# Pacing the weight-sum transfers of a recurrence stage, and issuing their copies from another engine

## The chip, the core and the metric

The kernel runs on one core of a Trainium2 chip. The metric is the device time of one execution in microseconds. The kernel before was timed three times: 2056.03, 2061.7 and 2062.01 us, median 2061.7 us.

## The reference

Two layers work on 1024 tokens of 1024 channels. The first layer mixes tokens with a gated linear recurrence (HGRN2) of eight heads, the second with a causal convolution; each is followed by a squared-ReLU MLP, and every step ends in a scaled residual and a layer norm. The part that matters here is the recurrence and the MLP's second weight:

```
q = silu(x @ Wq);  f = lb + (1-lb)*sigmoid(x @ Wf);  k = 1-f;  v = x @ Wv
S_t = diag(f_t) S_{t-1} + k_t v_t^T;    o_t = S_t^T q_t          # per head, 128 x 128 states
o = o * rsqrt(mean(o^2) + eps) * norm_g                          # per head and token
o = o * silu(x @ Wg);  mix = o @ w_out
x = layer_norm(ALPHA*x + mix)
x = layer_norm(ALPHA*x + square(relu(x @ w1)) @ w2)
```

## The kernel before

Matrices are multiplied in float32 by splitting each operand into a high and a low part (three matmuls for one), and large products are done by a seven-product scheme on 2 x 2 blocks, which needs sums and differences of the weight's blocks beside the blocks themselves. The second MLP weights `w2` of both layers are cut into 16 pieces of four 128 x 1024 blocks (`to_sum`, L427). For each piece `block_sums` (L399 to L426) makes four sums in DRAM with transfers alone, and they are read back as weight forms much later (`form`, L429, from 871.6 us on in the trace).

For a piece that is summed during the recurrence stage there are five transfers, all issued by GpSimd. Two plain copies of 1 MB put blocks into the four sum places (L419 and L420). An adding transfer of 1 MB (L421) adds two more blocks onto the first two places, and so needs the first copy to have landed. Two adding transfers of 512 KB (both L423) add one sum place onto the next, so each needs the transfer before it. A transfer that needs another waits for it on GpSimd, at its issue, and what GpSimd has behind it in its order waits too. With `gap=12` the five are recorded at ticks 0, 6, 12, 24 and 36.

The order of work in this stage is written out by the code itself (`manual_schedule`, L372): the engines' instructions stand in the order in which the Python code issues them. Twelve pairs of weight columns, seven block products each (the loop at L1007), make 84 products of 12 matmuls. `pair_product` calls `slot` after every three matmuls; `slot` calls `tick` (L390), which counts one tick and runs the jobs that `later` (L384) has put down for it. So a tick is a step of recording, not a time. `make_form` (L587) prepares weight forms in `fs` about three products ahead: ScalarE rounds to the high part, VectorE subtracts. `evacuate` (L824) empties a product's PSUM bank, on ScalarE by `COPY t<-ps` for three of the seven; the bank of such a product is next written one product later at the earliest.

Between products, `step` (L883) advances up to two of the eight heads through `recurrence(h)` (L634). Its last steps matter here. `outer` and `chain` make the states, `attend` leaves a head's output in PSUM in two halves (`out_ps`), and `settle(half)` (L731) normalises one: four squares with sums on ScalarE (`o,ss<-ps`, L735), two small instructions on GpSimd (`ss`, L736 and L518: scale and add, then the power -1/2), and four ticks later four scalings on ScalarE (`o<-ps,ss`, L741). `give(half)` (L746) then turns the half with four transposes on TensorE (`ps<-ident,o`) and stores it. So each half of each head makes a round ScalarE, GpSimd, ScalarE, TensorE, and GpSimd's part stands in one order with the sum transfers.

SyncE issues all other loads and stores of the stage, among them 256 KB weight blocks (`pr`, L585). In the main loop a new piece of `to_sum` is begun when `(7 * p + ORDER.index(i)) % 6 == 1`, every sixth product, as long as more than four pieces are left (L1022 and L1023): twelve pieces. The other four are done later, two from L1442 and two from L1774.

Of the kernel before, what the change touches and what calls it, by code (L numbers as in the profile page):

```python
# [12 lines left out]
ALU = mybir.AluOpType  # L13
# [21 lines left out]
NPAR = TAP + KB * TAPS  # L35

KBYTES = 220
PAIRS = [("q", 0), ("q", 1), ("q", 2), ("q", 3), ("g", 0), ("q", 4), ("q", 5), ("q", 6), ("g", 1), ("q", 7), ("g", 2), ("g", 3)]
NPOOL = (12, 11)
SEQ = "P00 P01 P02 P03 P04 P05 P06 P07 P10 P11 P12 P13 N0 P14 F0 P15 S0 P16 P17 UA0 UA1 E2 E3 N1 E4 F1 E5 E6 S1 E7 UB0 UB1 L2 L3 L4 L5 L6 L7"  # L40
# [4 lines left out]
ORDER = (1, 2, 6, 5, 7, 3, 4)  # L45
# [223 lines left out]
def body(ctx, tc, d, out):  # L269
    nc = tc.nc  # L270
# [109 lines left out]
    vd = [[dram.tile([P, NTB, HT], F32, name=f"vd{m}{n}") for n in range(2)] for m in range(2)]  # L380

    ticks, waiting = [0], []

    def later(n, job):  # L384
        if n:
            waiting.append((ticks[0] + n, job))
        else:
            job()

    def tick(n=1):  # L390
        for _ in range(n):
            ticks[0] += 1
            for at, job in [w for w in waiting if w[0] <= ticks[0]]:
                waiting.remove((at, job))
                job()

    sums = {}

    def block_sums(name, layer, c, after=None, gap=0, adds=None):  # L399

        t = sums[name, layer, c] = dram.tile([4, P, 1024], F32, name=f"sum_{name}{layer}{c}")
        v, w = t.rearrange("a p n -> p a n"), d[name][layer, c].rearrange("a p n -> p a n")
        queue = nc.sync if after is not None else nc.gpsimd
        if adds is not None:

            def copies(rows, after):
                nc.sync.dma_start(out=t[0:4:2, rows.start, 0:1], in_=after)
                queue.dma_start(out=v[rows, 0:2], in_=w[rows, 0:4:2])
                queue.dma_start(out=v[rows, 2:4], in_=w[rows, 0:2])

            copies(slice(16, P), after)
            adds.append(lambda after: copies(slice(0, 16), after))
            adds.append(lambda after: nc.gpsimd.dma_start(out=v[:, 0:2], in_=w[:, 2:4], accum_op=ALU.add))
            for i in (2, 3):
                adds.append(lambda after, i=i: nc.gpsimd.dma_start(out=v[:, i], in_=v[:, i - 1], accum_op=ALU.add, max_dma_last_dim=4096))
            return
        if after is not None:
            nc.sync.dma_start(out=t[0:4:2, 0, 0:1], in_=after)
        queue.dma_start(out=v[:, 0:2], in_=w[:, 0:4:2])  # L419
        later(gap // 2, lambda: queue.dma_start(out=v[:, 2:4], in_=w[:, 0:2]))  # L420
        parts = [lambda: nc.gpsimd.dma_start(out=v[:, 0:2], in_=w[:, 2:4], accum_op=ALU.add)]  # L421
        for i in (2, 3):
            parts.append(lambda i=i: nc.gpsimd.dma_start(out=v[:, i], in_=v[:, i - 1], accum_op=ALU.add, max_dma_last_dim=4096))  # L423
        for i, part in enumerate(parts):
            later((i + 1) * gap, part)

    to_sum = [(*of, c) for of in (("w2", 0), ("w2", 1)) for c in range(NFC)]  # L427

# [72 lines left out]
    for k in range(4):  # L501
        c = slice((k % 2) * HT, (k % 2 + 1) * HT)
# [118 lines left out]
    qk, gates, vts = {}, {}, {}  # L621
# [12 lines left out]
    def recurrence(h):  # L634
# [71 lines left out]
        for n in (32, 64):  # L706
            for s in range(0, n2, 2 * n):
                c, r = divmod(s, P)
# [61 lines left out]
        def outer(cs):  # L770
            for c in cs:
                tensor.matmul(state_ps[:, c % NTB], kt[:, c, :], values(c), start=True, stop=True)
# [10 lines left out]
        def attend(cs):  # L783
            for c in cs:
                tensor.matmul(out_ps[:, c, :], A[:, c, :], values(c), start=True, stop=c == 0)
                if c:
                    tensor.matmul(out_ps[:, c, :], Q[:, c * P : (c + 1) * P], states[c], start=False, stop=True)

        outer(range(NTB))
        later(1, lambda: chain(range(NTB)))  # L790
        yield
# [2 lines left out]
        later(1, lambda: (chain(range(NTB, nk)), settle(0)))  # L794
        yield
        attend(range(NTB, 2 * NTB))
        later(1, lambda: settle(1))
        if h < H - 2:
            for half in range(2):
                load_values(2 * h + 2 + half)  # L800
# [108 lines left out]
    to_load, loaded, to_gate = [], [], []  # L909
# [96 lines left out]
    tick(4)  # L1006
    for p, (kind, j) in enumerate(PAIRS):  # L1007
        st = {"banks": dict(turn_of)}
        turn_of = {"z": turn_of["a"], "a": turn_of["b"], "b": turn_of["z"]}
        pace[1] = 0.0 if p == 0 else 0.6 if p < 3 else 0.5  # L1010
        if kind == "g" and p < len(PAIRS) - 1:
            to_load += [(2 * j, 0), (2 * j + 1, 1), (2 * j, 1), (2 * j + 1, 0)]
        if p == len(PAIRS) - 1:
            seam()
        for i in ORDER:
            if kind == "q" and i == 2:
                while any(a[0] <= j - 3 for a in active) or recs and recs[0] <= j - 3:
                    tick()
                    step()
            pair_product(p, i, made.pop(0), st)  # L1020
            later(2, make_form)
            if (7 * p + ORDER.index(i)) % 6 == 1 and len(to_sum) > 4:  # L1022
                block_sums(*to_sum.pop(0), gap=12)  # L1023
        if kind == "q":
            later(4, lambda j=j: recs.append(j))
    early_out = ((0, 0), (1, 0), (2, 0))
# [7 lines left out]
    while step():  # L1034
        tick()
    tick(100)
    assert not waiting and not loaded and not to_load and not gates, (waiting, gates)
    order.close()
    oT = [o[0] for o in oT]

# [145 lines left out]
    class Up:  # L1186
# [14 lines left out]
        def settle(self, c):  # L1201

            for q in range(2):
                self.first(self.of[c], q)
# [415 lines left out]
    rest, adds = [None, None], []  # L1620
# [303 lines left out]
```

## Time and profile before

| what | value |
|---|---|
| median of three runs | 2061.7 us |
| span of the profiled execution | 2068.3 us |
| TensorE busy | 2031.0 us, 98% of the span |
| VectorE, ScalarE, GpSimd busy | 72%, 53%, 19% |
| granted TensorE clock, mean | 0.997 |
| recurrence stage, first to last sum transfer issued by GpSimd | 73.86 to 393.81 us |
| DMA busy share of 16 engines, 200 to 300 us | 0.93 |

The profile gives the profiled execution's span and no other time of it; that span is 6.6 us over the median of the runs that were timed. In the rows of the profile a bracket at a row's end is the time the engine sat idle before it and what ended that. PE is TensorE, PEld its weight loads, DVE VectorE, ACT ScalarE, POOL GpSimd, and SPq the queue of transfers that SyncE issues.

### The profile page before, as it was taken

What the parts mean: (1) busy time and instruction counts of PE and PEld (TensorE: products, weight loads), DVE (VectorE), ACT (ScalarE), POOL (GpSimd) and SP (SyncE); (2) the same over time, 40 slices, a digit from 0 to 9 for tenths busy, and PEclk for the clock granted to TensorE, in tenths of its full rate; (3) what the DMA queues carried; (4) which work ended last, traced back from release to release, by engine and by line L of the source; (5) the groups of instructions that cost most, each with busy time, mean ns of one, the idle gap of its engine ahead of it and who ended that gap; (6) DMA issues with size and microseconds to landing.
All of it is one profiled execution on the core that took longest, in us unless ns stands there. A gap on an engine that the chain in (4) does not pass through costs nothing. (4 is left out here: it accounts for less than half of the span.)

```text
span 2068.3 us, 29719 instructions
## 1 busy us (share of the span) xinstructions
PE 2031.0 (98%) x11192; PEld 1674.5 (81%) x11192; DVE 1482.9 (72%) x1976; ACT 1090.2 (53%) x1727; POOL 388.4 (19%) x387
## 2 busy tenths in 40 slices
PE   8999999999999999999999999999999999999998
PEld 7888777788888888888888888888878878888886
DVE  8698877877775666565567898889589666755556
ACT  5456555641464555444444776488625555343333
POOL 0112222111001000000001699079210000100002
PEclk9999999999999999999999999999999999999999
DMA  4778889852689786999998855587759778996542
GB/s 186 224 195 233 238 224 270 254 189 81 187 288 298 243 295 221 353 341 332 335 349 292 309 193 185 190 323 271 256 215 339 245 232 291 386 292 204 193 155 102
DMA packets 183944, 517.55 MB, mean 250 GB/s; under 512 B 17912, under 2 KB 49784, under 8 KB 182776
## 3 DMA queue, kind: packets, MB, share of 16 engines
q1 hardware_dynamic: 168312, 456.93, 62.6%
q0 software_dynamic: 15488, 58.72, 12.3%
q8 instruction: 87, 1.43, 0.3%
q14 instruction: 57, 0.47, 0.1%
HBM read 380.85 MB, written 201.85 MB: 282 GB/s over the span
## 5 line engine op out<-in xcount | busy, mean ns | idle before, releaser
L204 PE MATMUL ps<-dw,dh 128*128 128x512 f32 x2688 | 611.6, 389 | 1.9 <-ACT dh L72 1.1
L204 PEld LDWEIGHTS ps<-dw,dh 128*128 128x128 f32 x2688 | 504.1, 188 | 107.2 <-ACT dh L72 1.6
L204 PE MATMUL ps<-x1f,fw 128*128 128x512 f32 x1344 | 309.3, 390 | 2.3 <-DVE c L204 1.2
L204 PEld LDWEIGHTS ps<-x1f,fw 128*128 128x128 f32 x1344 | 251.1, 188 | 56.2 <-ACT c L1224 2.3
L204 PE MATMUL ps<-xf,fs 128*128 128x512 f32 x1008 | 249.3, 398 | 4.1 <-issue 1.9
L204 POOL TENSOR_TENSOR cb<-cb,prod 128x512 f32<-128x512 f32 x168 | 222.7, 1334 | 12.9 <-ACT prod L1555 2.3
L204 DVE TENSOR_TENSOR dh<-dh 128x1024 fp32r<-128x1024 f32 x112 | 136.4, 1222 | 117.3 <-ACT dh L72 117.1
L204 PEld LDWEIGHTS ps<-xf,fs 128*128 128x128 f32 x1008 | 184.5, 189 | 43.4 <-issue 2.1
L204 DVE SCALAR_TENSOR_TENSOR ps<-u,par,ps 128x512 f32<-128x512 f32 x296 | 206.2, 750 | 11.0 <-ACT ps L1567 9.5
L72 ACT CAST dh<-dh 128x1024 fp32r<-128x1024 f32 x112 | 117.4, 1051 | 163.7 <-DMA dh<-hf 163.7
L204 PE MATMUL ps<-xa,wa 128*128 128x512 f32 x864 | 203.1, 392 | 0.1
L204 PEld LDWEIGHTS ps<-xa,wa 128*128 128x128 f32 x864 | 160.3, 188 | 33.3 <-ACT ha L1289 0.3
L204 DVE TENSOR_TENSOR dw<-dr,dw 128x1024 fp32r<-128x1024 f32 x112 | 136.2, 1222 | 66.6 <-ACT dw L72 65.9
L72 ACT CAST dw<-dr 128x1024 fp32r<-128x1024 f32 x112 | 117.0, 1051 | 119.2 <-PE ps L204 100.2
L1555 ACT ACTIVATE prod<-u,par 128x512 f32<-128x512 f32 x168 | 119.8, 726 | 36.6 <-POOL cb L204 35.7
L518 POOL TENSOR_TENSOR mv<-mv,nhalf 128x1 f32<-128x1 f32 x32 | 43.3, 1355 | 407.6 <-DVE mv L204 407.6
L1408 POOL COPY next<-ss 128x1 f32<-128x1 f32 x38 | 21.2, 558 | 413.8 <-DVE spare L204 265.1
L204 PE MATMUL ps<-xb,wa 128*128 128x512 f32 x384 | 91.1, 393 | 0.0
L204 PE MATMUL ps<-w,oT 128*128 128x512 f32 x384 | 89.5, 391 | 1.3 <-ACT oT L932 0.8
L204 DVE TENSOR_TENSOR spare<-next,spare 128x1024 fp32r<-128x1024 f32 x38 | 46.5, 1224 | 60.6 <-ACT spare L1401 60.5
L204 PE MATMUL ps<-vw,xf 128*128 128x512 f32 x336 | 79.8, 399 | 6.0 <-ACT vw L435 5.2
L204 PEld LDWEIGHTS ps<-w,oT 128*128 128x128 f32 x384 | 71.5, 188 | 16.6 <-ACT oT L932 1.2
(236 smaller groups left out, 2959.6 us busy)
## 6 DMA issues: line engine op xcount, KB each, us to landing
wa<-ready SPq DMA_DIRECT2D x140, 512.0 KB, 5.5
dh<-hf SPq DMA_DIRECT2D x112, 512.0 KB, 5.3
sum_w<-in_w_dram POOLq DMA_DIRECT2D x40, 1024.0 KB, 10.9
ready<-spare SPq DMA_DIRECT2D x76, 512.0 KB, 4.6
raw<-in_w1q_dram SPq DMA_DIRECT2D x66, 512.0 KB, 4.4
dr<-sum_w SPq DMA_DIRECT2D x64, 512.0 KB, 5.7
hf<-ht SPq DMA_DIRECT2D x112, 256.0 KB, 4.9
dr<-in_w_dram SPq DMA_DIRECT2D x48, 512.0 KB, 5.3
```

The costliest lines, as they stand in the source:

```text
L72: self.nc.scalar.copy(out=slot[:, 0, c], in_=raw[:, c])
L204: return op(*args, **kw)
L518: nc.gpsimd.tensor_tensor(out=dst, in0=src, in1=nhalf[:, :n], op=ALU.pow)
L1408: nc.gpsimd.tensor_copy(out=raw[:, :1], in_=now)
L1555: nc.scalar.activation(tp, u[:, k : k + HT], AF.Copy, scale=tap(j, k))
```

## The change

Three things change in the recurrence stage, for the twelve pieces that are begun there.

First, both copies of a piece are issued by ScalarE in place of GpSimd, one right behind the other. Second, a piece's four parts (the pair of copies, the 1 MB add, and the two 512 KB adds) stand in one list, `adding`. At the end of every tick `add_some` issues at most one part: the first piece in the list whose own last part was at least 16 ticks ago (`SPACE`), and only if any piece's last part was at least 4 ticks ago. Third, nothing is issued while `quiet[0]` is above zero. It goes up when a head comes to `outer` and down right after its second `settle`, so no sum transfer is recorded between the two `ss` pairs of a head or shortly ahead of the first. A new piece is put on the list every fifth product in place of every sixth.

```diff
+SPACE = 16
...
     ticks, waiting = [0], []
+    adding, quiet, added = [], [0], [0]
...
                 waiting.remove((at, job))
                 job()
+            add_some()
+
+    def add_some():
+        for one in adding:
+            if not quiet[0] and one[0] <= ticks[0] and added[0] <= ticks[0]:
+                one.pop(1)()
+                one[0], added[0] = ticks[0] + SPACE, ticks[0] + SPACE // 4
+                if len(one) == 1:
+                    adding.remove(one)
+                break
...
-        queue.dma_start(out=v[:, 0:2], in_=w[:, 0:4:2])
-        later(gap // 2, lambda: queue.dma_start(out=v[:, 2:4], in_=w[:, 0:2]))
-        parts = [lambda: nc.gpsimd.dma_start(out=v[:, 0:2], in_=w[:, 2:4], accum_op=ALU.add)]
+
+        def copies():
+            copier = nc.scalar if turns else queue
+            copier.dma_start(out=v[:, 0:2], in_=w[:, 0:4:2])
+            copier.dma_start(out=v[:, 2:4], in_=w[:, 0:2])
+
+        parts = [copies, lambda: nc.gpsimd.dma_start(out=v[:, 0:2], in_=w[:, 2:4], accum_op=ALU.add)]
...
-        for i, part in enumerate(parts):
-            later((i + 1) * gap, part)
+        if turns:
+            adding.append([ticks[0], *parts])
+        else:
+            for part in parts:
+                part()
...
+        quiet[0] += 1
         outer(range(NTB))
...
-        later(1, lambda: settle(1))
+        later(1, lambda: (settle(1), quiet.append(quiet.pop() - 1)))
...
-            if (7 * p + ORDER.index(i)) % 6 == 1 and len(to_sum) > 4:
-                block_sums(*to_sum.pop(0), gap=12)
+            if (7 * p + ORDER.index(i)) % 5 == 1 and len(to_sum) > 4:
+                block_sums(*to_sum.pop(0), turns=True)
```

The instructions of TensorE, VectorE and SyncE stand in the same order as before. On GpSimd 24 copies are gone and the adds stand elsewhere; on ScalarE 24 copies are new. The lines of the new kernel are 14 to 20 higher.

GpSimd around the normalising of the fourth head, before. L421 and L423 are adds, L419 and L420 copies; the number in a name is that of the piece.

```order
L419 DMA sum_w_2457<-in_w_dram 128x2x1024
L420 DMA sum_w_2457<-in_w_dram 128x2x1024
L736 TENSOR_SCALAR ss<-ss 128x4
L518 TENSOR_TENSOR ss<-ss,nhalf 128x4
L423 DMA sum_w_2229<-sum_w_2229 128x1024
L421 DMA sum_w_2457<-in_w_dram 128x2x1024
L736 TENSOR_SCALAR ss<-ss 128x4
L518 TENSOR_TENSOR ss<-ss,nhalf 128x4
L423 DMA sum_w_2457<-sum_w_2457 128x1024
```

The same place in the new program (L437 and L439 are the adds, L755 and L537 the two `ss` instructions).

```order
L439 DMA sum_w_1687<-sum_w_1687 128x1024
L439 DMA sum_w_1965<-sum_w_1965 128x1024
L437 DMA sum_w_2127<-in_w_dram 128x2x1024
L755 TENSOR_SCALAR ss<-ss 128x4
L537 TENSOR_TENSOR ss<-ss,nhalf 128x4
L755 TENSOR_SCALAR ss<-ss 128x4
L537 TENSOR_TENSOR ss<-ss,nhalf 128x4
L439 DMA sum_w_1965<-sum_w_1965 128x1024
L439 DMA sum_w_2127<-sum_w_2127 128x1024 x2
```

The copies have left, the four `ss` instructions stand together, and two adds that stood between the pairs now stand ahead of the first or behind the second.

ScalarE while the second head is normalised, before, from the squares of its second half to the lay-out of the next head's scores (`at<-blocks`).

```order
L735 ACTIVATE o,ss<-ps 128x128 x4
L837 COPY t<-ps 128x512
L614 CAST fs<-pr 128x512
L741 ACTIVATE o<-ps,ss 128x128 x4
L754 ACTIVATE kt<-ps,nrm 128x512
L614 CAST fs<-pr 128x512
L821 ACTIVATE sq<-t 128x512
L754 ACTIVATE kt<-ps,nrm 128x512
L837 COPY t<-ps 128x512
L614 CAST fs<-pr 128x512
L837 COPY t<-ps 128x512
L665 COPY at<-blocks 32x8x32 x4
```

The same place in the new program, up to the first copy of the piece after; the second half's squares stand right ahead of it.

```order
L434 DMA sum_w_1687<-in_w_dram 128x2x1024
L435 DMA sum_w_1687<-in_w_dram 128x2x1024
L857 COPY t<-ps 128x512
L633 CAST fs<-pr 128x512
L760 ACTIVATE o<-ps,ss 128x128 x4
L773 ACTIVATE kt<-ps,nrm 128x512
L633 CAST fs<-pr 128x512
L841 ACTIVATE sq<-t 128x512
L773 ACTIVATE kt<-ps,nrm 128x512
L857 COPY t<-ps 128x512
L633 CAST fs<-pr 128x512
L434 DMA sum_w_1965<-in_w_dram 128x2x1024
```

Two pairs of copies came in, eleven rows apart. The program counts the transfers of SyncE and ScalarE on eight semaphores (`DMAHW0` to `DMAHW7`), and a transfer that takes a semaphore first waits until the transfer that had it last has landed. The second of these pairs again, with what its rows wait for:

```order
L633 CAST fs<-pr 128x512 [waits DMAHW2_49]
L434 DMA sum_w_1965<-in_w_dram 128x2x1024 [waits DMAHW5_49]
L435 DMA sum_w_1965<-in_w_dram 128x2x1024 [waits DMAHW7_49]
L857 COPY t<-ps 128x512 [waits PE_49]
L684 COPY at<-blocks 32x8x32 [waits DVE_49]
```

The first copy of piece 1687 holds `DMAHW5`, so the first copy of piece 1965 waits on ScalarE until that copy has landed, and `COPY t<-ps` waits behind it. The same can be seen between the pieces 2558 and 2804 after the fourth head, where both copies of 2804 follow both of 2558 on the semaphores `DMAHW4` and `DMAHW5`; the copies of 2410 and of 2558, in turn, stand only three rows apart. Between the copies of 2558 and those of 2804 stand five products, between those of 1687 and of 1965 three. The other pairs wait for nothing, for transfers of SyncE that stand far ahead of them, or for a copy that stands six products ahead.

More of the change, by code (lines that the diff above doesn't have):

```diff
@@ L395, in tick, with block_sums @@
                 job()
+            add_some()
[7 more added lines that the diff above has]
+                break
     sums = {}
-    def block_sums(name, layer, c, after=None, gap=0, adds=None):
+    def block_sums(name, layer, c, after=None, turns=False, adds=None):
         t = sums[name, layer, c] = dram.tile([4, P, 1024], F32, name=f"sum_{name}{layer}{c}")
@@ L1036, in body @@
     tick(100)
-    assert not waiting and not loaded and not to_load and not gates, (waiting, gates)
+    assert not waiting and not loaded and not to_load and not gates and not adding, (waiting, gates, adding)
     order.close()
```

## Prediction

> **What bounds the kernel now.** I read the page first, then TensorE's waits over the stage, the table of stretches, and the timelines of GpSimd, ScalarE and TensorE around each head.
>
> ```profile
> PE 2031.0 (98%) x11192; PEld 1674.5 (81%) x11192; DVE 1482.9 (72%) x1976; ACT 1090.2 (53%) x1727; POOL 388.4 (19%) x387
> ```
>
> TensorE sets the time: a microsecond is won only where TensorE idles or runs slow. Outside the recurrence stage the orders of TensorE, VectorE and SyncE don't change, so I count that stage alone. In stretches of 50 us it reads:
>
> ```profile
> 200.00:250.00 50.00, 47.68 (x502) 38.69 (x502) 41.15 (x68) 31.21 (x73) 13.62 (x14) 1.00 0.93 261
> 250.00:300.00 50.00, 45.04 (x462) 37.25 (x461) 37.47 (x60) 27.44 (x65) 11.30 (x14) 0.97 0.93 238
> 300.00:350.00 50.00, 48.04 (x619) 40.78 (x618) 43.15 (x75) 27.06 (x71) 10.87 (x14) 1.00 0.90 245
> 350.00:400.00 50.00, 45.63 (x463) 37.64 (x462) 39.26 (x66) 31.04 (x82) 11.80 (x16) 0.97 0.88 218
> ```
>
> Behind the length stand the busy times of PE, PEld, DVE, ACT and POOL, then the granted clock, the DMA share and GB/s. The second and fourth stretch lose most, and there alone the clock is 0.97. What TensorE waited for, in total, times and longest:
>
> ```profile
> PE ps L204 <- ACT o L741: 7.8, 4, 4.9
> ...
> PE ps L204 <- issue: 1.9, 1, 1.9
> ```
>
> `ACT o L741` is the scaling of a head's output. One such wait, seen on the three engines (start, length, idle before it):
>
> ```profile
> 263.46 0.23 ACT L735 ACTIVATION_READ_ACCUMULATOR o<-ps 128x1 f32 x1
> ```
>
> ```profile
> 262.32 0.92 POOL L423 DMA_DIRECT2D sum_w<-sum_w  x1 [2.25 <-DMA sum_w<-sum_w]
> 269.47 1.22 POOL L421 DMA_DIRECT2D sum_w<-in_w_dram  x1 [6.23 <-issue]
> 270.77 0.19 POOL L736 TENSOR_SCALAR ss<-ss 128x4 f32<-128x4 f32 x1
> 271.04 1.03 POOL L518 TENSOR_TENSOR ss<-ss,nhalf 128x4 f32<-128x4 f32 x1
> ```
>
> ```profile
> 272.11 1.14 ACT L741 ACTIVATE o<-ps,ss 128x128 f32<-128x128 f32 x4 [6.09 <-POOL ss L518]
> ```
>
> ```profile
> 273.30 1.12 PE L204 MATMUL ps<-ident,o 128*128 128x128 f32 x4 [4.86 <-ACT o L741]
> ```
>
> The squares were done at 263.69, but GpSimd took them up at 270.77, since L421 stood ahead and waited for a copy. The same happens at 350 and 388:
>
> ```profile
> 349.14 1.20 POOL L421 DMA_DIRECT2D sum_w<-in_w_dram  x1 [7.12 <-issue]
> ...
> 388.04 0.86 POOL L423 DMA_DIRECT2D sum_w<-sum_w  x1 [11.37 <-DMA sum_w<-in_w_dram]
> ```
>
> ```profile
> 353.40 1.09 PE L204 MATMUL ps<-xf,fs 128*128 128x512 f32 x4 [1.86 <-issue]
> ...
> 391.50 0.66 PE L204 MATMUL ps<-ident,o 128*128 128x128 f32 x4 [2.27 <-ACT o L741]
> ```
>
> ```profile
> 352.19 1.14 ACT L741 ACTIVATE o<-ps,ss 128x128 f32<-128x128 f32 x4 [3.16 <-POOL ss L518]
> ```
>
> The wait of 1.86 is put down to nothing, but it ends at 353.40, 0.07 after that scaling ends at 353.33, and the transposes of `o` stand next; I count it in. (This and the idle of PEld are one wait, not two.)
>
> **The gain, part by part.** Holding the adds while a head is normalised puts the four `ss` instructions of a head side by side, with no add between. Where GpSimd was free, the round costs TensorE nothing:
>
> ```profile
> 317.30 0.60 PE L204 MATMUL ps<-ident,o 128*128 128x128 f32 x4
> ```
>
> So the waits of 7.8 and 1.9 go, 9.7 us. With them goes slow running: 0.03 of the busy 45.04 and 45.63 us is 2.7. The Trainium skill, "TensorE: Matmul & The Clock Gate", section "Part 1: The HAM clock gate", has the clock halved after an idle window of about 3.4 us. By it only the wait of 4.86 would cost clock, an estimate of 1.7 us in place of 2.7; the 0.97 beside waits no longer than 2.27 disagrees, and the row decides. Together 12.4. I take off a tenth, because VectorE was busy 43.15 of 50 us in the stretch with the least disturbance and will be late now and then: **11.0 us**.
>
> The 24 copies leave GpSimd; it is busy at most 13.62 of 50 us, so its issue time itself (about 1.0 us each, below) is worth nothing beyond the waits above. With 16 ticks between the parts of a piece, in place of 12, an add finds its predecessor landed more often. What is late next is what bounds TensorE between the waits: VectorE and ScalarE, at 1 to 2 us in 50.
>
> **The costs.** No row shows ScalarE issuing a transfer. The nearest are SyncE's and GpSimd's copies of the same kind (ns minimum, median, maximum):
>
> ```profile
> L419 POOL DMA_DIRECT2D sum_w<-in_w_dram x12: 889/1028/1612, 73.9 to 361.9; - x12
> L420 POOL DMA_DIRECT2D sum_w<-in_w_dram x12: 728/1014/1394, 74.7 to 362.6; - x12
> L408 SPq DMA_DIRECT2D sum_w<-in_w_dram x4: 550/571/627, 1387.1 to 1796.8; - x4
> L409 SPq DMA_DIRECT2D sum_w<-in_w_dram x4: 590/684/1392, 1387.8 to 1798.1; - x4
> ```
>
> I take SyncE's, since the program counts both engines' transfers on the same semaphores: 0.57 + 0.68 = 1.25 us a pair, at most 1.61 + 1.39 = 3.0. Twelve pairs are 15 us of an engine that is busy 27 to 31 of 50 us. How long such a transfer takes to land under this load:
>
> ```profile
> DMA to landing us min/median/max: 5.2/9.7/14.5
> ```
>
> That is for all sum transfers between 100 and 400 us. Two pairs must wait on ScalarE for earlier copies. First the copies of piece 1965 after the second head; in the trace of before their neighbours stand so:
>
> ```profile
> 189.73 0.63 ACT L837 COPY t<-ps 128x512 f32<-128x512 f32 x1
> ...
> 196.60 0.64 ACT L614 CAST fs<-pr 128x512 fp32r<-128x512 f32 x1
> 199.19 0.59 ACT L837 COPY t<-ps 128x512 f32<-128x512 f32 x1 [1.95 <-PE ps L204]
> ```
>
> Piece 1687 is issued at 189.7 and lands at 199.4, at most 204.2. ScalarE comes to 1965 at 197.2, is held 2.2 us (at most 7.0), issues for 1.25, and empties the bank at 200.7 instead of 199.19, 1.5 late (at most 6.3). Behind the held copies stand that emptying and the rounding of the next forms. TensorE needs the bank one product later:
>
> ```profile
> 318.52 3.02 PE L204 MATMUL ps<-xf,fs 128*128 128x512 f32 x12
> ```
>
> A product of 3.0 less the emptying of 0.6 leaves 2.4 us of cover: nothing is lost at 1.5, 3.9 at 6.3. I take 0.5, near the median's end. Second the copies of 2804:
>
> ```profile
> 279.21 0.59 ACT L837 COPY t<-ps 128x512 f32<-128x512 f32 x1 [1.92 <-PE ps L204]
> ...
> 298.97 1.06 ACT L684 COPY kd<-qk 128x1024 f32<-128x1024 f32 x1
> ```
>
> Four copies go out together by 279.2, twice what went out at once before, so the last lands after about twice 9.7 us, at 298.6 (at most at 308.2). ScalarE gets there at 300.0: held 0, at most 8.2. The same cover makes that a loss of 0 to 7. I take 1.0, nearer the median's end. The other ten pairs are 12.5 us on ScalarE. Rows like the two with 1.95 and 1.92 idle before them hide a whole pair; where none stands near, part of 1.25 shows. I take 1.5, from 0 to 6.
>
> Starting a piece every fifth product makes the early stage denser in transfers at a DMA share that is 0.93 already. SyncE's weight blocks could suffer:
>
> ```profile
> DMA to landing us min/median/max: 2.6/7.2/12.0
> ```
>
> Forms are made three products ahead, about 9 us of cover, and the sum transfers end no earlier than before since the hold stretches them; I take nothing, up to 4.
>
> Costs are 0.5 + 1.0 + 1.5 = 3.0 us (0 to 21). Net 11.0 - 3.0 = **8.0 us** of the profiled 2068.3, 0.4%. That span is 6.6 over the median of the timed runs, and I take the difference over unchanged: 2061.7 - 8.0 = **2053.7 us**. With no cost and the whole 12.4 it would be 2049.3.
>
> **The rivals.** *The waits come back in another place.* The hold is counted in recording steps. Two adds stand right ahead of the fifth head's `ss`, and both need copies of the four that went out together. Against it is the time between the hold's start and the squares' end, as at the fourth head:
>
> ```profile
> 251.96 1.05 PE L204 MATMUL ps<-v,kt 128*128 128x128 f32 x8
> ```
>
> ```profile
> 258.26 0.22 ACT L735 ACTIVATION_READ_ACCUMULATOR o<-ps 128x1 f32 x1
> ```
>
> From `outer` to the last square pass 6.5 us, in which an add can be waited for at no cost. For it: an add was seen to wait 11.37 us. If one wait like that at 270 returns, 4.86 and 1.4 of clock, the gain is 8.0 - 6.3 = 1.7 and the time 2060.0, no change that a measurement of this kernel can tell (0.3%, 6.2 us). The Trainium skill, "DMA: Bandwidth & Descriptors", section "Issuing engines are not separate DMA queues", speaks for this rival: transfers of all engines run on the same 16 DMA engines, and issuing from another saves only the issue time. By that rule no copy lands sooner, and only the places of the waits change. The share of 0.93 agrees that there is no room to land sooner. That the waits shown are those of one profiled execution and smaller in the timed ones leads to the same place.
>
> *ScalarE becomes the engine that is held.* Its price is the upper ends above: 3.9 at piece 1965, 7.0 at 2804, 6.0 for the other pairs and 1.4 of clock for one long wait, 18.3 us. Against 11.0 that is 7.3 slower, 2069.0. It decides from a loss of 17.2 us on. For it: these waits are in the program and the landing times reach 14.5. Against it: it needs the upper end everywhere, and ScalarE gets back idle time in which it waited for GpSimd (6.09 and 3.16 above).
>
> That the change doesn't do what it says I rule out from the order: the `ss` instructions do stand together.
>
> **How the numbers follow.** The forecast, faster by 6.2 to 12.4 us (2049.3 to 2055.5), gets 0.55; no change, 0.29; ScalarE held, 0.16. The range takes in the forecast whole and most of the middle case: 2048 to 2066, which leaves out about 0.2, most of it above.
>
> **What would show it.** Right: TensorE's wait for the scaling of `o` falls from 7.8 to under 2 us, the clock reads 1.00 in every stretch between 200 and 400 us, and no add stands between a head's squares and its `ss`. Also, ScalarE's copies take 0.5 to 0.7 us each, and ScalarE idles before the copies of 1965 and 2804 by about 2 and 0 us. Wrong: waits of TensorE for `t<-ps` or `fs` that sum to over 5 us, a wait of `ss` for an add ahead of a head, or the stage gone faster and the time given back before 450 us.

## The result, and the profile after

| | median us | runs | ratio to before, 95% interval |
|---|---|---|---|
| before | 2061.66 | 2056.03 to 2062.01 | |
| changed | 2086.96 | 2083.31 to 2088.79 | 1.0122 (1.0107 to 1.0136) |

The change makes the kernel slower by 25.3 us, 1.2%. The forecast of 2053.7 us and its range, 2048 to 2066, were wrong. The profiled execution of the changed kernel is the one of 2083.31 us, the fastest of its four, with a span of 2081.5.

What the change was for did happen. TensorE's waits over the stage (0 to 580 us: in total, times, longest) show next to nothing for the scaling of `o` (L760 here), where it was 7.8 before:

```profile
PE ps L205 <- ACT kt L743: 12.9, 1, 12.9
PE ps L205 <- DVE state L205: 6.7, 2, 3.4
...
PE ps L205 <- ACT t L857: 4.2, 1, 4.2
...
PE ps L205 <- ACT o L760: 0.3, 1, 0.3
```

In its place the rows of `kt`, `state` and `t` have grown, four waits of 23.8 us together. The table of stretches, with the same columns as before, shows where, and that the clock goes down with them:

```profile
150.00:200.00 50.00, 46.29 (x593) 38.93 (x592) 37.27 (x66) 31.05 (x87) 12.96 (x15) 0.97 0.76 208
200.00:250.00 50.00, 36.70 (x416) 30.25 (x415) 32.10 (x52) 21.13 (x54) 7.23 (x8) 0.86 0.73 199
...
300.00:350.00 50.00, 46.53 (x484) 38.60 (x483) 36.94 (x62) 28.16 (x65) 8.87 (x9) 0.93 0.96 273
350.00:400.00 50.00, 45.77 (x473) 38.50 (x472) 41.17 (x67) 28.00 (x65) 7.77 (x9) 0.97 0.76 194
```

A good yardstick for the stage is the start of TensorE's first output projection behind it. Before, and then changed:

```profile
421.91 0.73 PE L204 MATMUL ps<-w,oT 128*128 128x512 f32 x2 [0.77 <-ACT oT L932]
```

```profile
437.92 0.73 PE L205 MATMUL ps<-w,oT 128*128 128x512 f32 x2 [0.77 <-ACT oT L952]
```

The stage is 16.0 us longer in these two executions, and behind it nothing is lost (the spans differ by 13.2). Against a second profile of the kernel before, in which this row starts at 410.07, it is 27.9; more on that execution below. The longest wait can be followed through four engines. First ScalarE, with its queue (ACTq) (start, length, idle before it): two pairs of copies, 4 MB, within 8.6 us, the first held back until the second head was normalised.

```profile
192.38 0.56 ACTq L434 DMA_DIRECT2D sum_w<-in_w_dram  x1
...
192.97 0.64 ACTq L435 DMA_DIRECT2D sum_w<-in_w_dram  x1
...
200.33 0.56 ACTq L434 DMA_DIRECT2D sum_w<-in_w_dram  x1
...
200.93 0.64 ACTq L435 DMA_DIRECT2D sum_w<-in_w_dram  x1
...
226.26 0.62 ACT L633 CAST fs<-total 128x512 fp32r<-128x512 f32 x1 [13.78 <-DVE total L205]
...
230.72 0.97 ACT L743 COPY kt<-ps 128x512 f32<-128x512 f32 x2
```

Around the second pair SyncE asks for two weight blocks (`pr`). VectorE waits for the first until 224.11, 28.5 us after its issue, and for the second until 225.49; TensorE waits for `kt`, which ScalarE reaches late:

```profile
195.56 0.33 SPq L604 DMA_DIRECT2D pr<-in_wp_dram  x1
...
199.07 0.33 SPq L604 DMA_DIRECT2D pr<-in_wp_dram  x1
```

```profile
224.11 0.69 DVE L205 TENSOR_TENSOR pr<-pr 128x512 f32<-128x512 f32 x1 [11.69 <-DMA pr<-in_wp_dram]
225.49 0.69 DVE L205 TENSOR_TENSOR total<-pr 128x512 f32<-128x512 f32 x1 [0.68 <-DMA pr<-in_wp_dram]
```

```profile
231.35 2.07 PE L205 MATMUL ps<-v,kt 128*128 128x128 f32 x8 [12.92 <-ACT kt L743]
```

The landing row of these blocks between 180 and 240 us has 26.3 as its longest, that of the second block (the trace has the landing of about half of these transfers, and not that of the first). Before, 12.0 was the longest of the stage, and 13.9 in the second profile:

```profile
DMA to landing us min/median/max: 2.6/3.2/26.3
```

What moved meanwhile: the queues between 199 and 225 us (packets, MB, share of the 16 engines' time; q0 is GpSimd's, q1 SyncE's, q10 ScalarE's), first of the changed kernel, then a stretch of before of the same length with the transfer engines nearly as full, 191 to 217 us:

```profile
DMA  9999999899999999999999999999899999999997
...
q0 software_dynamic: 704, 2.62, 54.4%
q10 hardware_dynamic: 714, 2.72, 27.0%
q1 hardware_dynamic: 1560, 1.85, 22.1%
```

```profile
DMA  9899999999989999999999999999989799999974
...
q0 software_dynamic: 1156, 4.37, 66.8%
q1 hardware_dynamic: 2352, 2.88, 34.2%
```

In these two stretches SyncE's queue got 1.85 MB in 26 us, 71 GB/s, and 2.88 MB, 111 GB/s. It had work all the time in the first, as the two blocks show. But the two numbers make no rule: other full stretches of 26 us show 68 GB/s with two queues (the second profile of before, from 243 us) and 132 with three (ScalarE's copies alone, from 204 us).

The second loss (`state`, 3.4 of the 6.7 us) begins with ScalarE's idle 4.89 us at the copies of piece 2804. It waits at each of them for an earlier copy to land, 0.7 us until 312.24 and 3.0 us until 315.81, and comes late to the cast behind them, and VectorE and TensorE after it. The landing row of all second copies has 26.6 us as its longest, which is the copy that ends this wait.

```profile
312.24 0.56 ACTq L434 DMA_DIRECT2D sum_w<-in_w_dram  x1
315.81 0.56 ACTq L435 DMA_DIRECT2D sum_w<-in_w_dram  x1
316.41 0.62 ACT L633 CAST fs<-total 128x512 fp32r<-128x512 f32 x1 [4.89 <-DMA sum_w<-in_w_dram]
```

```profile
DMA to landing us min/median/max: 9.6/14.5/26.6
```

The two others (`state`, 3.3 us, ending at 184.10, and `t`, 4.2, ending at 358.59) follow on waits of ScalarE for SyncE's store of a head's output. Before, one such wait of 1.5 us stood in the stage.

```profile
178.25 0.48 ACT L743 COPY kt<-ps 128x384 f32<-128x384 f32 x1 [3.91 <-DMA od<-kt]
...
356.63 0.48 ACT L743 COPY kt<-ps 128x384 f32<-128x384 f32 x1 [5.60 <-DMA od<-kt]
```

### The profile page after: what moved, and what is told of

It is laid out like the page before. It is cut to its first block, busy times and chain, and to the rows that moved or that the text cites. A ratio compares the mean times of both kernels' runs of the same rounds, so it can differ in the third digit from the quotient of the medians.

```text
span 2081.5 us, 29718 instructions
## 1 busy us (share of the span) xinstructions
PE 2035.5 (98%) x11192; PEld 1681.4 (81%) x11192; DVE 1484.2 (71%) x1976; ACT 1092.0 (52%) x1727; POOL 370.1 (18%) x363
## 4 chain that ended last, share of the span: by engine, by line
PE 67%; DMA 14%; DVE 8%; ACT 4%; issue 4%; POOL 2%; SPq 0%; ACTq 0%; DVEq 0%; POOLq 0%
PE ps L205 67%; DMA pr<-in_wp_dram 2%; DMA sum_w<-in_w_dram 1%; DMA next<-in_wpw_dram 1%; POOL cb L205 1%; DMA next<-in_w1q_dram 1%; DMA dr<-in_w_dram 1%; DMA raw<-in_w1q_dram 1%; DMA od<-kt 1%; DMA hf<-ht 1%; DMA next<-in_w_dram 1%; DMA dh<-hf 1%; DVE spare L205 1%; DMA vr<-in_wv_dram 1%; ACT hr L1219 1%
## 5 line engine op out<-in xcount | busy, mean ns | idle before, releaser
L537 POOL TENSOR_TENSOR mv<-mv,nhalf 128x1 f32<-128x1 f32 x32 | 42.2, 1321 | 407.7 <-DVE mv L205 407.7
```

The source lines that it names most:

```text
L537: nc.gpsimd.tensor_tensor(out=dst, in0=src, in1=nhalf[:, :n], op=ALU.pow)
```

## The experiments

Four theories were put to the test. A: ScalarE stands at its copies and its own work comes late. B: the copies come in bunches and crowd SyncE's small loads and stores. C: the copies' bytes on a queue of their own do that. D: it is the load, or where a full stretch meets a small transfer. The runs were made in four groups, each with its own runs of before; their medians are 2057.36, 2059.62, 2059.26 and 2060.74, so across groups the ratios are compared and not the medians. 0.1% is 2 us.

| kernel | median us | ratio, 95% interval |
|---|---|---|
| changed, copies issued by GpSimd | 2068.38 | 1.0055 (1.0035 to 1.0075) |
| before, copies issued by ScalarE | 2064.03 | 1.0027 (1.0012 to 1.0042) |
| changed, no hold | 2078.54 | 1.0104 (1.0084 to 1.0123) |
| changed, every sixth product | 2088.19 | 1.0146 (1.0128 to 1.0164) |
| changed, second copy six ticks later | 2075.38 | 1.0075 (1.0054 to 1.0096) |
| ScalarE's copies at old places, adds alone held | 2068.75 | 1.0048 (1.0029 to 1.0067) |
| changed, adds left out | 2053.81 | 0.9974 (0.9964 to 0.9984) |
| before and few bytes issued by ScalarE | 2058.33 | 0.9996 (0.9986 to 1.0006) |
| before, every seventh product | 2070.92 | 1.0047 (1.0034 to 1.0060) |
| changed, copies by GpSimd, no hold | 2072.02 | 1.0050 (1.0036 to 1.0065) |
| changed, again | 2084.67 | 1.0118 (1.0101 to 1.0135) |
| changed, one pair of copies later | 2079.00 | 1.0090 (1.0072 to 1.0108) |
| before, evenly spaced, GpSimd | 2063.05 | 1.0014 (1.0003 to 1.0025) |
| the same, copies by ScalarE | 2070.92 | 1.0051 (1.0036 to 1.0066) |
| before, other phase | 2063.78 | 1.0016 (1.0005 to 1.0027) |

**The copies back on GpSimd.**

```diff
-            copier = nc.scalar if turns else queue
+            copier = queue
```

> The changed kernel, with the copies issued by GpSimd again; list, hold and spacing stay. Theory A (the issuing engine: ScalarE stands at its own copies for the time of issuing and for transfers ahead of them, and what it does next for the recurrence comes late): ScalarE's waits for sum_w (4.9 us ahead of fs) are gone and the time falls from 2087 to 2065 or less. Theory B (bunches: both copies of a block at one moment, and two blocks within 8.5 us after a head's hold, crowd SyncE's small loads and stores, whoever issues them): SyncE's weight block that took 26.3 us still takes 15 or more, VectorE still waits for it, and the time stays at 2080 to 2090. If both have a share it lies at 2068 to 2078.

1.0055: more than half of the loss is gone, so who issues the copies counts, and something else does too. The weight blocks land in 10.6 us at the most. But TensorE's wait for the scaling of `o` is 7.8 us again, in an execution that is the slowest of its four (2073.39). At 316 us GpSimd, ScalarE and TensorE read:

```profile
316.23 0.71 POOL L435 DMA_DIRECT2D sum_w<-in_w_dram  x1 [8.37 <-issue]
317.01 0.19 POOL L755 TENSOR_SCALAR ss<-ss 128x4 f32<-128x4 f32 x1
```

```profile
318.34 1.14 ACT L760 ACTIVATE o<-ps,ss 128x128 f32<-128x128 f32 x4 [13.60 <-POOL ss L537]
```

```profile
319.54 1.11 PE L205 MATMUL ps<-ident,o 128*128 128x128 f32 x4 [7.43 <-ACT o L760]
```

GpSimd stood 8.4 us at the second copy of a pair, for nothing that the profile names, with the `ss` steps behind it. The list keeps that wait, since the hold doesn't take back a copy that stands ahead of it in GpSimd's order.

**ScalarE's copies alone.**

```diff
+        copier = nc.scalar if gap else queue
-        queue.dma_start(out=v[:, 0:2], in_=w[:, 0:4:2])
+        copier.dma_start(out=v[:, 0:2], in_=w[:, 0:4:2])
-        later(gap // 2, lambda: queue.dma_start(out=v[:, 2:4], in_=w[:, 0:2]))
+        later(gap // 2, lambda: copier.dma_start(out=v[:, 2:4], in_=w[:, 0:2]))
```

> The kernel before, with one part of the change alone: ScalarE issues the copies of the recurrence's sums, at their old places (the second six ticks behind the first), adds and the sixth product as before. Theory A (issuing engine): slower than before by 8 us or more, with ScalarE idle at its copies. Theory B (bunches): the transfers lie as before, so the time is within 0.3% of 2061.7, at most 2 us up for 16 x 2 issues of 0.6 us.

1.0027, between the two expectations: this part alone costs some 5.5 us, and by itself not the 25.

**No hold.**

```diff
-        quiet[0] += 1
-        later(1, lambda: (settle(1), quiet.append(quiet.pop() - 1)))
+        later(1, lambda: settle(1))
```

> The changed kernel without the hold: the list and its spacing stay, but a head's normalising no longer stops it. Theory B as first put (the hold piles two blocks up behind it): the copies come one block at a time, the loads of 20 us and over are gone, 10 to 20 us of the loss of 25 come back, and TensorE's wait for the scaling of o returns to some 5 us: 2068 to 2078. Theory A: nothing changes but the place: 2083 to 2091. If both copies together (2 MB at once) are enough for the crowding, whatever the hold does, it also stays at 2080 to 2090.

1.0104. The hold is not what costs most: without it the interval still overlaps that of the changed kernel. Nor does the hold make the gain: TensorE's wait for `o` is 0.3 us without it as well, against the expectation, though in the fastest of the four executions (2071.61). With its copies elsewhere GpSimd stands 126 us at its sum transfers between 100 and 480 us, where it was 196 in the first profile of before.

**Every sixth product.**

```diff
-            if (7 * p + ORDER.index(i)) % 5 == 1 and len(to_sum) > 4:
+            if (7 * p + ORDER.index(i)) % 6 == 1 and len(to_sum) > 4:
```

> The changed kernel with a sum begun at every sixth product, as before, and not at every fifth; list, hold, spacing and ScalarE's copies stay. Theory D (density: what hurts is that as many bytes move in five sixths of the time): 2065 to 2072. Theories A and B: one or two of the three long stalls may fall elsewhere, but most stay: 2075 to 2090.

1.0146: the sums spread wider, and no better. Density by itself falls. The long waits stand at other places (10.3 for `kt`, 6.9 for `t`, 5.0 for `f`).

**The second copy of a pair later.**

```diff
-            copier.dma_start(out=v[:, 2:4], in_=w[:, 0:2])
+            later(6 if turns else 0, lambda: copier.dma_start(out=v[:, 2:4], in_=w[:, 0:2]))
```

> The changed kernel, with a block's second copy six ticks behind its first, as before, and not in the same moment; ScalarE still issues both, list, hold, spacing and fifth product stay. If the pair of copies (2 MB at once beside the adds) makes the long landings: most of the 25 us come back, 2062 to 2070. If the pieces of two blocks behind a hold are what fills the transfer engines, whether a pair is split or not: 2078 to 2090.

1.0075: the pair at one moment is worth about 0.45%, 9 us, of the loss, and not most of it. Theory B holds in part.

**Held adds without the rest.**

```diff
-            adding.append([ticks[0], *parts])
+            copies()
+            adding.append([ticks[0] + 12, *parts[1:]])
...
-            copier.dma_start(out=v[:, 2:4], in_=w[:, 0:2])
+            later(6 if turns else 0, lambda: copier.dma_start(out=v[:, 2:4], in_=w[:, 0:2]))
...
-            if (7 * p + ORDER.index(i)) % 5 == 1 and len(to_sum) > 4:
+            if (7 * p + ORDER.index(i)) % 6 == 1 and len(to_sum) > 4:
```

> The two parts that may be worth having, without the rest: ScalarE issues a block's copies at their old places (at once, and six ticks later), a sum starts at every sixth product, and only the three adding transfers stand in the list with its hold and spacing. Beside the run in which ScalarE's copies alone were changed (0.3% slower than before) it tells what list and hold of the adds do by themselves. If holding the adds is worth the waits for the scaling of o: 2050 to 2058. If held adds come out in a bunch and crowd the weight blocks by themselves: 2070 or more.

1.0048 beside 1.0027 with ScalarE's copies alone. The list and its hold give nothing even here, where they have the adds alone; the two intervals overlap, so a small loss by them isn't shown either.

**No adds.**

```diff
-            adding.append([ticks[0], *parts])
+            adding.append([ticks[0], copies])
```

> The changed kernel with the adding transfers of the recurrence left out (the sums are then not made; 2 of its 5 MB per block are never moved), all copies where they were. If the copies alone, on ScalarE and in pairs, cause the loss, by holding ScalarE or by crowding: 2075 or more. If it takes copies and adds together to fill the transfer engines for 20 us and longer: 2050 or less, with SyncE's weight blocks landing in 10 us at the most.

This kernel leaves out the adds and so doesn't make the sums. 0.9974, 5.4 us faster than before, with the copies in pairs, on ScalarE, and held, as in the changed kernel. TensorE's waits and the landing of the weight blocks (100 to 430 us):

```profile
PE ps L205 <- ACT kt L743: 0.5, 1, 0.5
...
PE ps L205 <- ACT o L760: 0.3, 1, 0.3
```

```profile
DMA to landing us min/median/max: 2.5/2.9/9.8
```

So pairs on ScalarE do no harm that shows where half of the sums' bytes are missing (2 of 4 MB a block, not of 5 as the expectation has it). It takes copies and adds together. This time also says how little there was to win: with GpSimd never in the way and the transfer engines with less to do it is 5.4 us (3.3 to 7.4 by the interval). It is no strict bound, since the pairs on ScalarE are still in it.

**Before, once more,** unchanged, for one time and a second profile.

> The kernel before, unchanged: a second profiled execution of it, since the first spanned 2068.3 us and its timed runs were 2056 to 2062. If the waits for the scaling of o (7.8 us in the first profile) are a trait of the program, they are 6 to 9 here as well; if they were that one execution's, 0 to 4, and the change had little to win.

This execution took 2052.98 us, its span was 2051.2, and the waits read:

```profile
PE ps L204 <- DVE state L204: 1.5, 2, 0.9
...
PE ps L204 <- ACT t L837: 0.9, 1, 0.9
...
PE ps L204 <- ACT o L741: 0.6, 2, 0.3
```

So the 7.8 us that the change set out to remove are no fixed trait of the program. But this execution is faster than every timed run of before (2054.61 at the least), so 0.6 is not the usual size either. The kernel of the next experiment has GpSimd's instructions in the same order, and its profiled execution is an ordinary one (2058.52): it has 3.0 us for `o` and 2.0 put down to nothing, 5.0 where the first profile had 9.7.

**Few bytes by ScalarE.** The kernel before with, in addition,

```diff
+            s = dram.tile([4, P, 8], F32, name=f"few_{name}{layer}{c}").rearrange("a p n -> p a n")
+            nc.scalar.dma_start(out=s[:, 0:2], in_=w[:, 0:4:2, 0:8])
+            later(gap // 2, lambda: nc.scalar.dma_start(out=s[:, 2:4], in_=w[:, 0:2, 0:8]))
```

> The kernel before, and beside it ScalarE issues for every block of the recurrence, at the places where it issued its copies in the second experiment, two transfers of as many rows but only 32 bytes each into a scratch tensor; the sums' copies stay with GpSimd. If it was the issuing (ScalarE standing 0.6 us for each, and the order of the shared semaphores) that cost 0.3% there, as much is lost here: 2063 to 2067 where the kernel before is at 2059. If it was the copies' bytes on a queue of their own, beside GpSimd's and SyncE's: 2057 to 2061.

0.9996 (0.9986 to 1.0006): issuing costs nothing, or 0.06% at the most. It takes ScalarE as long as the copies do, 0.56 us for the first of a pair, 0.56 in the changed kernel:

```profile
L423 ACTq DMA_DIRECT2D few_w<-in_w_dram x11: 559/559/560, 106.0 to 348.1; - x11
```

Theory A falls, except for the holds that a late landing makes; those are a consequence.

**Every seventh product, kernel before.**

```diff
-            if (7 * p + ORDER.index(i)) % 6 == 1 and len(to_sum) > 4:
+            if (7 * p + ORDER.index(i)) % 7 == 1 and len(to_sum) > 4:
```

> The kernel before with a sum begun at every seventh product and not at every sixth: the same twelve sums, spread wider, nothing else. With no adds at all 6 us were won, so at most that can come; if the load of the transfer engines in the recurrence is what costs, a seventh less of it gives 1 to 4 us: 2055 to 2058 where before is at 2059. If the sums' end, now some 12 products later, runs into the stage behind: 2062 or more.

1.0047, slower with a lighter load, as the expectation has it for sums that run into the work behind: the last add is issued at 436.06, before at 393.81. In the profile nearly all of the loss is in one stretch, and most of it is one wait, with ScalarE waiting for the store of a head's output:

```profile
400.00:450.00 50.00, 38.09 (x172) 31.46 (x171) 26.43 (x34) 23.50 (x49) 5.30 (x7) 0.86 0.95 316
```

```profile
407.93 0.48 ACT L724 COPY kt<-ps 128x384 f32<-128x384 f32 x1 [6.05 <-DMA od<-kt]
```

```profile
408.95 2.05 PE L204 MATMUL ps<-f,kt 128*128 128x128 f32 x8 [7.90 <-ACT t L837]
```

**The list on GpSimd without the hold.**

```diff
-            copier = nc.scalar if turns else queue
+            copier = queue
...
-        quiet[0] += 1
-        later(1, lambda: (settle(1), quiet.append(quiet.pop() - 1)))
+        later(1, lambda: settle(1))
```

> The changed kernel with GpSimd issuing the copies and without the hold: of the change there are left the list with its spacing, the pair of copies at one moment, and the fifth product. With the hold this was 0.55% slower than before. If the hold is what costs (idle transfer engines, then a bunch): within 0.2% of before. If pairs and the fifth product cost: 2065 to 2072.

1.0050, where it was 1.0055 with the hold. Hold or not makes no difference here either; what is left of the list (pairs at one moment, spacing of 16, fifth product) costs 0.5%. GpSimd has a part in it: TensorE waits 9.9 us for `o`, in an execution at the median. And GpSimd stands 63.7 us, in ten waits, at the second copy of a pair (51.0 in ten with the hold); before, with the second copy six ticks later, it has no such wait.

**The changed kernel again.**

> The changed kernel unchanged, on the chip of the others here, with a second profile: slower by 1.1 to 1.4% as before; if its long waits hang on where the bunches fall, they stand at the same three places (a weight block near 200 us, a copy that holds ScalarE near 290 to 315, the store of kt near 340 to 355); if they are chance, elsewhere.

1.0118, and the waits come back to within 0.6 us:

```profile
PE ps L205 <- ACT kt L743: 12.3, 1, 12.3
PE ps L205 <- DVE state L205: 6.4, 2, 3.5
...
PE ps L205 <- ACT t L857: 4.1, 1, 4.1
```

They are a trait of this order, as the full 7.8 us for `o` before were not.

**One pair of copies later,** the changed kernel otherwise.

```diff
-            adding.append([ticks[0], *parts])
+            adding.append([ticks[0] + (8 if (layer, c) == (0, 6) else 0), *parts])
```

> The changed kernel with one step of it moved: the sixth block's pair of copies is issued eight places later in the list, so that it no longer stands 8 us behind the pair of the fifth block; no other instruction moves. If these two pairs make the weight block issued at 199 us land 26 us later: it lands in 15 us or less, TensorE's wait of 12 us ahead of kt is down to 5 or less, and the time falls by 6 to 13 us, to 2071 to 2079. If the load over the whole stretch does it, wherever a pair stands: the wait stays or stands some us further on, and the time stays at 2083 to 2089.

1.0090, some 6 us better, though the intervals overlap, and the profile is that of the fastest execution (2075.71 of up to 2084.78). The longest landing of the weight blocks between 180 and 240 us is halved while their median goes up from 3.2 to 9.7, and the wait of 12.9 us is 0.5; part of it comes back at `state`:

```profile
DMA to landing us min/median/max: 5.4/9.7/13.3
```

```profile
PE ps L205 <- DVE state L205: 12.6, 3, 6.0
...
PE ps L205 <- ACT t L857: 4.1, 1, 4.1
...
PE ps L205 <- ACT kt L743: 0.5, 1, 0.5
```

That two pairs 8 us apart made these blocks late is shown by what the move did to them; that spreading one pair mends the stage is not so.

**Evenly spaced, by GpSimd and by ScalarE.** The kernel before with

```diff
-        later(gap // 2, lambda: queue.dma_start(out=v[:, 2:4], in_=w[:, 0:2]))
+        later(5 if gap else 0, lambda: queue.dma_start(out=v[:, 2:4], in_=w[:, 0:2]))
...
-            later((i + 1) * gap, part)
+            later((14, 34, 43)[i] if gap else 0, part)
```

> The kernel before, its five transfers of a block (GpSimd, every sixth product) set so that over the blocks one falls every 5 ticks: copies at 0 and 5, adds at 14, 34 and 43, where before they stood at 0, 6, 12, 24, 36, so that a copy and an add of three blocks met at one tick. If bunches are what makes the small transfers late: 2052 to 2057 where before is at 2059, nearly the time without adds. If it is the load of the whole stretch: within 0.2% of before. If the order in GpSimd's queue (a copy now lies ahead of an older block's add) holds the squares' sums: 2062 or more.

The second kernel has in addition

```diff
+        copier = nc.scalar if gap else queue
-        queue.dma_start(out=v[:, 0:2], in_=w[:, 0:4:2])
+        copier.dma_start(out=v[:, 0:2], in_=w[:, 0:4:2])
-        later(5 if gap else 0, lambda: queue.dma_start(out=v[:, 2:4], in_=w[:, 0:2]))
+        later(5 if gap else 0, lambda: copier.dma_start(out=v[:, 2:4], in_=w[:, 0:2]))
```

> The same even places, with ScalarE issuing the copies. If a queue of their own gives the copies more of the transfer engines at the cost of SyncE's small transfers, even when they don't come in bunches: slower than the run beside it by 3 us or more. If only bunches count: within 2 us of it.

1.0014 and 1.0051. Even places don't beat the old ones. At the same places ScalarE's copies cost 0.37% more. The store of a head's output (KB each, median us to landing, 100 to 450 us) comes later, GpSimd's copies first, then ScalarE's:

```profile
od<-kt SPq DMA_DIRECT2D x14, 256.0 KB, 8.2
```

```profile
od<-kt SPq DMA_DIRECT2D x14, 256.0 KB, 12.2
```

**Another phase.**

```diff
-            if (7 * p + ORDER.index(i)) % 6 == 1 and len(to_sum) > 4:
+            if (7 * p + ORDER.index(i)) % 6 == 4 and len(to_sum) > 4:
```

> The kernel before, with every block of sums begun three products later (fourth of six, not first): the same transfers at the same distances, moved by some 12 us against the heads. If what counts is how many bytes stand there at a time: within 0.2% of before. If it counts which of the heads' small transfers meets a full stretch: another time, by 0.3% or more, to either side.

1.0016 (1.0005 to 1.0027). That is within the 0.2% of the first expectation and short of the 0.3% of the second, though the interval leaves out 1: the phase counts, but for some 3 us.

**What follows together.** Four pairs differ only in who issues the copies. The last two pairs were run in different groups. Beside each ratio stands the longest landing of a weight block in its profile (100 to 430 us); where there are two profiles, both:

| places of the copies | GpSimd | ScalarE | difference | longest landing, GpSimd | ScalarE |
|---|---|---|---|---|---|
| as before | 1 | 1.0027 | 0.27% | 12.0 and 13.9 | 12.3 |
| even | 1.0014 | 1.0051 | 0.37% | 11.4 | 17.0 |
| list, no hold | 1.0050 | 1.0104 | 0.54% | 10.0 | 24.6 |
| list and hold | 1.0055 | 1.0122 | 0.67% | 10.6 | 26.3 and 25.7 |

ScalarE costs in each, and by these numbers more under the list, where the copies come in pairs, though the intervals don't set 0.27 and 0.54 apart. It isn't its time (few bytes: nothing). It is the copies' bytes issued by it, together with those of the adds. In three of the four pairs the longest landing of SyncE's blocks goes up with it; in the first, which costs least, it doesn't. The medians hardly move (5.9 to 7.7 us in all ten profiles).

How the bytes do it is not shown. Two accounts stay: a third queue takes a share from SyncE's, or copies that no longer stand behind the adds in GpSimd's order lie closer together in time. The Trainium skill, "DMA: Bandwidth & Descriptors", section "Queues, rings and completion order", says that each transfer engine takes its queues in turn, packet by packet. By that rule an estimate of SyncE's part is a half with two queues and a third with three, if all have work. No run here shows it: 111 and 71 GB/s would fit, 68 and 132 don't, and it isn't known that all queues had work throughout in those stretches.

## Why the prediction was wrong

The step that failed is the last of the costs: "SyncE's weight blocks could suffer", "I take nothing, up to 4". It was by far the largest term.

- **The costs, weight blocks.** A block took 26.3 us to land, against a cover put at "about 9 us", and cost TensorE 12.9. With the three other waits, of which one begins with copies that landed late and two with stores of SyncE, for which the prediction has no term at all, it is 23.8 us. The clock costs more: 0.03 of 46.29, 0.14 of 36.70, 0.07 of 46.53 and 0.03 of 45.77 us are 11.2. Together with the 0.3 for `o` that is 35.3. Before, the waits for `o`, "issue", `t`, `state` and `kt` were 7.8, 1.9, 1.4, 1.4 and 0.5, in total 13.0, and 2.7 of clock, 15.7. The difference, 19.6, is 3.6 more than the 16.0 by the stage's end; the clock by stretches is the loose term in it. In the second profile of before the same rows are 0.6, 0.3, 0.9, 1.5 and 0.5, with no clock lost; there the difference is 31.5, against 27.9 by the stage's end. The reason I gave, that the hold stretches the sums' transfers, speaks of bytes per stage. What counted was which engine issued the copies, and at which moment they stood beside the adds, and for that I had no row: no trace of before has a third queue at work.
- **The upper bound.** "Up to 4" was no bound. No row is given for it; it is about what the longest landing of before, 12.0, leaves over the cover. Nothing in the trace kept landing from getting worse.
- **The gain.** The waits went as forecast: 7.8 fell to 0.3, the four `ss` steps stand together, and the wait of 1.9 is gone. That the hold did it is not shown, since without it the 0.3 is the same. Its size was wrong. 11.0 us was read from an execution that was a bad one: its span was 2068.3, over every timed run of before; another was 2051.2 with 0.6 us of that wait, and without any adds 5.4 us were won. "I take the difference over unchanged" failed here: a wait that comes in some executions is not carried over whole. My first rival said as much, and its reading of it was right as far as the gain goes. Its price (2060.0) was not, since it left out the loss.
- **ScalarE's time.** 0.56 and 0.64 us a copy, forecast 0.57 and 0.68. At piece 1965 it was not held (forecast about 2 us), at 2804 by 0.7 and 3.0 (forecast 0, at most 8.2), since the last of the four copies ahead took 26.6 us to land and not "about twice 9.7". The ten other pairs were put at 1.5 us; with few bytes the cost is nothing. Rival two came to the right sign by a cause that made one of the four waits: it priced a held engine, at 18.3 us, and its 2069.0 is 18 us short of the time.
- **The rule on issuing engines, cited with the first rival.** I used it to say that no copy lands sooner and only the places of the waits change. It says nothing on whose transfers land later, and I did not ask: what SyncE's transfers lose had no price in the sum or in a rival, beyond the "up to 4".
- **What was to show it.** `o` under 2 us: right. No add between squares and `ss`: right. Clock 1.00 from 200 to 400 us: wrong. Waits for `t` and `state` over 5 us: they came, and the largest stands at `kt`, which I had not named.

Open stays how ScalarE's bytes make SyncE's transfers late, by shares or by coming closer together. Open is also why the list on GpSimd costs 0.5%. The profiles show GpSimd held at the second copies of pairs, ahead of `ss`; pairs, spacing and the fifth product weren't separated there. What the hold adds to ScalarE's pairs is 0.18%, with intervals that overlap. And none of the kernels that make the whole result is shown to be faster than before; the best of those that put the sums' transfers elsewhere, the one with even places, is 0.14% slower.

## What to carry to other kernels

Where transfer engines are full, moving a large transfer to another engine's queue doesn't only move its issue: here it cost time in all four pairs. Price it by the small transfers on which the compute engines wait, by their longest landing and not by the median. And before a wait of one profiled execution is taken as a gain, set its span beside the timed runs: the one used here lay 0.3% above their median and had waits that other executions didn't have, or had smaller.

## What the runs showed of the hardware that was not expected

- The same program had 7.8 us of a wait in one execution and 0.6 in another, with spans of 2068.3 and 2051.2 us; the changed kernel's two profiles agree to 0.6 us in every long wait (spans 2081.5 and 2081.2).
- With ScalarE's copies and GpSimd's adds under way a block of 256 KB took 26.3 us to land; with the same copies and no adds the longest of the stage took 9.8.
- The second of two `sum_w` copies in a row held GpSimd by up to 8.4 us at its issue, ten times in a stage, with nothing that the profile shows it to wait for.
- One wait of TensorE of 12.9 us goes with a granted clock of 0.86 over its 50 us, and one of 7.9 (seventh product), with another of 2.7 behind it, with 0.86 as well. In the first profile of before a wait of 2.27 us, which ends at 391.50, is followed by a granted clock of 0.50 from 392.5 to 395.5 us.
